# Start addresses of TensorE's operands, plain tiles in halves, and the scan's fp32 steps regrouped

## The chip, the cores and the metric

One core of a Trainium2 chip runs the whole program. The metric is the device time of one execution in microseconds (us); the kernel before took 1315.77, 1312.59 and 1308.76 us in three runs, median 1312.59. TensorE (PE) multiplies a *stationary* operand (128x128, brought in by a weight load, PEld) with a *moving* operand (128 rows by up to 512 columns), VectorE is DVE, ScalarE is ACT, GpSimd is POOL, and SyncE (SP) issues most DMAs.

## The reference

The kernel computes one Mamba-2 layer and a final RMSNorm for 512 tokens and a model width of 2048. DEPTH is 1, so the pooling mixer never runs. Cut to what matters:

```python
hn   = rmsnorm(x, ln_g)                       # (512, 2048)
proj = hn @ w_in                              # 2048 -> 10304: z (4096), x/B/C (6144), dt (64)
xbc  = silu(causal_depthwise_conv(xbc, conv_w, conv_b))      # 4 taps
dt   = softplus(dt + dt_bias);  a = -exp(a_log)
y    = ssd_chunked_scan(xs * dt, dt * a, B, C)               # 64 heads of 64, 8 groups, state 128
y    = rmsnorm((y + d_skip * xs) * silu(z), norm_g)          # over 4096
out  = rmsnorm(x + y @ w_out, final_g)                       # 4096 -> 2048
```

Everything is float32.

## The kernel before

**Splitting.** Each large product is made of fp32r matmuls. A float32 operand is split into `hi`, its fp32r rounding, made by ACT (line 85), and `lo`, the rest, made by DVE (line 86). A product takes three matmuls: hi with hi, hi with lo, lo with hi.

**Input projection.** The eight tiles of the first four pairs in `seq` ("plain") are computed directly. `mm_k` (line 192) does, for each of 16 k-tiles, three matmuls with a moving operand of 512 columns (`xh`, `xl`: the split, scaled input, all 512 tokens). The other 36 pairs of tiles go through `pair` (line 631), a Strassen-like scheme with seven products of half size. Each product (`product`, line 620) is 8 k-tiles times three matmuls with 256 moving columns; its stationary operand is a split sum of weight quarters (R11, T1, R22, T2, R21, T3, T4) and its moving operand is `xh`/`xl` or one of the forms `s` that `x_forms` makes. A pair takes QS = 28 steps, 4 to a product; the last product of a pair (T4) is returned as `last` and emitted inside the next pair, 8 steps in. The first pair has no predecessor, so nothing stands there.

**Output projection.** `opair` (line 842) does the same with y as the stationary operand (forms `f11`, `f1`, ...) and weights as the moving one, 256 columns, for two blocks of four; `mm_o` (line 881) does the rest with 512 moving columns, and the last of these stages takes its weights from the tiles named `f..` and `o..`.

**The scan** works on one unit (two heads) at a time, in fp32 matmuls and transposes between the products: `u_xt` (four transposes into the PSUM tile `tr`), `u_state` (into `yo`), `u_yd` (into `yd`, two halves of 64 columns of stationary), `u_yo` (fp32r, into `yo`), and per group of four units `g_bt` and `g_cb` (two score blocks into `tr`, masked by DVE at line 431). `tr`, `yd` and `yo` have one buffer each.

**What sets the order.** TensorE's, SyncE's and GpSimd's orders are written by hand: `run(step)` emits the functions that `add(step, f)` has put in the table `ev`, just before the matmuls of that step. The offsets are the numbers in `ramp`, in the default list `[28, 42, 56, 62, 65, 70]`, in `q_events` (loads, accumulating DMAs, splits) and in the `add` calls with `b0`. DVE's and ACT's orders come from a scheduler, with `urgent` raising a few instructions.

**Addresses.** Tiles stand in SBUF in the order in which their pools make them, padded to 32 bytes. In the built program the start addresses, modulo 256 bytes, are these:

| operands | moving | stationary | stationary minus moving | matmuls |
|---|---|---|---|---|
| `product`, 256 columns | 224 (`xh`, `xl`, `s`) | 0 (`hi`, `lo`, `h1h`, `h1l`) | 32 | 6048 |
| `oproduct`, 256 columns | 0 (`hi`, `lo`, `h1h`, `h1l`) | 224 (`f..`) | 224 | 1344 |
| `u_yo`, 256 columns | 32 | 32 | 0 | 96 |
| `mm_k`, 512 columns | 224 | 0 | 32 | 384 |
| `dt_mm`, 512 columns | 224 | 32 | 64 | 32 |
| `mm_o`, 512 columns | 0 or 224 | 0 or 224 | 0: 240, 32: 287, 224: 240 | 767 |

Adding whole k-tiles does not change the offset: their strides are multiples of 256 bytes.

Of the kernel before, what the change touches and what calls it, by code (L numbers as in the profile page):

```python
# [17 lines left out]
P = 128  # L18
L = 512
# [15 lines left out]
def mamba_layer(ctx: ExitStack, tc: tile.TileContext, d: dict, out: bass.AP):  # L35
# [14 lines left out]
    ph1 = ExitStack()  # L50
    sp = ph1.enter_context(tc.tile_pool(name="ssd", bufs=1))
    phx = ExitStack()
    xp = phx.enter_context(tc.tile_pool(name="xhat", bufs=1, side="right"))
# [112 lines left out]
    SSH = [P, 4, LH]  # L166
    xr = sp.tile([P, L + 3], F32, name="xr")

# [23 lines left out]
    def mm_k(ps, w, k8, k):  # L192
        hi, lo = w
        T.matmul(ps, hi[:, k8, :], xh[:, k, :], start=k == 0, stop=False)
        T.matmul(ps, hi[:, k8, :], xl[:, k, :], start=False, stop=False)
        T.matmul(ps, lo[:, k8, :], xh[:, k, :], start=False, stop=k == KT - 1)

# [153 lines left out]

    def dt_sums():
        pc = ps_tr.tile([P, NC, H], F32, name="tr")
        T.matmul(pc, tri, dts["a"], start=True, stop=True)
        with urgent():
            V.tensor_copy(out=cs, in_=pc)
        pl = ps_tr.tile([P, NC, H], F32, name="tr")
        T.matmul(pl, ones, dts["a"], start=True, stop=True)
        with urgent():
            V.tensor_tensor(out=nwl, in0=pl, in1=cs, op=ALU.subtract)  # L360
            V.tensor_tensor(out=win[:, 0, :], in0=nwl[:, 0, :], in1=pl[:, 1, :], op=ALU.add)
        V.tensor_copy(out=win[:, 1, :], in_=nwl[:, 1, :])
        S.activation(win, win, AF.Exp)
# [57 lines left out]
    def g_cb(g, i):  # L421
        if i == 0:
            gr[g]["cbm"] = sp.tile([P, 2, 3, P], F32, name="cbm")
        B, C = gr[g]["B"], gr[g]["C"]
        pcb = ps_tr.tile([P, 3, P], F32, name="tr")
        s0 = slice(i * 2 * P, i * 2 * P + P)
# [51 lines left out]
    def u_state(u):  # L478
# [3 lines left out]
        for c in range(2):  # L482
            T.matmul(pyo[:, 2, :], Bt[:, c, :], xw[:, c].rearrange("p h d -> p (h d)"), start=c == 0, stop=c == 1)
        with urgent():
            un[u]["sts"] = split(pyo[:, 2, :], [P, P], "sts")
# [116 lines left out]

    def q_events(n, b, last, e=0):
        for o, f, a in ((-38 - e, q_load, ("R11", 0, 0, "ra")), (-23 - e, q_split, ("R11", True)),
                        (-23 - e, q_fetch, ("T1", "R11", 0, 1)), (-3 - e // 2, q_split, ("T1",)),
                        (-12 - e // 2, q_load, ("R22", 1, 1, "rc")), (1 - e // 2, q_add, ("T2", "T1", "R22")),
# [24 lines left out]
    def pair(n, prev):  # L631
# [6 lines left out]
        W = lambda f: lambda: qs[n, f]  # L638
        product(s_, W("R11"), 11, True, b)
        A = ps_mm.tile([P, L], F32, name="mm")  # L640
        with urgent():
            S.copy(out=A[:, lo_], in_=s_)
        product(r_, W("T1"), 1, True, b + 4)
        with urgent():
            S.copy(out=sn[:, 1, :], in_=r_)  # L645
        if prev:
            prev(b + 8)
        else:
            for i in range(8, 12):
                run(b + i)  # L650
# [32 lines left out]
    for g in range(1, G):  # L683
        add(at["B", g] + (30 if ("B", g) in plain else 60), g_bt, g)
        for i in range(2):
            add(at["x", 4 * g] + 30 + 4 * i, g_cb, g, i)
    ramp = [[66, 71, 58, 75, 87, 92], [56, 65, 50, 68, 86, 92]]
    for u in range(NU):
        w = ramp[u] if u < len(ramp) else [28, 42, 56, 62, 65, 70]
        for o, f in zip(w, (u_load, u_decay, u_xt, u_state, u_yd, u_yo)):  # L690
            add(at["x", u] + o, f, u)
# [63 lines left out]
    add(b0 + 16, norm_b)  # L755
    add(b0 + 16, dt_mm)
    add(b0 + 44, g_bt, 0)
    add(b0 + 26, dt_softplus)
    add(b0 + 36, g_cb, 0, 0)
    add(b0 + 39, g_cb, 0, 1)  # L760
    add(b0 + 56, dt_sums)
    add(b0 + 62, dt_spread)

# [35 lines left out]
    def y_forms(i, j):  # L799

        n1, n2 = yraw.pop((i, j))
        if j == 0:
            for f in YF:
                yform[i, f] = [op.tile(QSH, F32R, name=f"f{f}{c}") for c in "hl"]
        jj = slice(2 * j, 2 * j + 2)
        t = fp.tile([P, 2, 2, LH], F32, name="yt")
# [35 lines left out]
    def opair(i, s, b, prev):  # L842
# [6 lines left out]
        q0, q1 = acc[:, 0:2, c[1]], acc[:, 2:4, c[1]]  # L849
        oproduct(s_, i, W("R11"), 11, True, b)  # L850
        A0 = ps_mm.tile([P, 2, LH], F32, name="mm")
        with urgent():
            S.copy(out=A0, in_=s_)
        oproduct(r_, i, W("T1"), 1, True, b + 4)
        with urgent():
            V.tensor_tensor(out=q1, in0=q1, in1=r_, op=ALU.subtract)
        if prev:
            prev(b + 8)
        else:
            for k in range(8, 12):  # L860
                run(b + k)
# [57 lines left out]
    for i, blk in enumerate(blocks):  # L919
        if type(blk) is tuple:  # L920
            for s in range(4):
                q_events(len(quads) + 4 * m + s, base[i] + s * QS, s == 3)
            for j in range(2):
# [33 lines left out]
    for kb, blk in enumerate(blocks[:-1]):  # L957
# [8 lines left out]
        for s, pairs in blk:  # L966
            ps = [None] * NC
            for p in pairs:
# [4 lines left out]
                for t in range(NC):  # L973
# [8 lines left out]
                    if p == pairs[-1]:  # L982
                        a = acc[:, t, s * L:(s + 1) * L]
                        with urgent():
                            if kb == 0 and 0 in pairs:
                                S.copy(out=a, in_=ps[t])
                            else:
                                V.tensor_tensor(out=a, in0=ps[t], in1=a, op=ALU.add)
                    if prev:
                        prev(step)  # L990
                        step += 4
                        prev = None
# [75 lines left out]
```

## Time and profile before

| | |
|---|---|
| three runs | 1315.77, 1312.59, 1308.76 us |
| profiled execution, span | 1310.4 us |
| PE busy | 1271.4 us (97%), 9548 matmul records |
| PEld busy | 1187.8 us (91%) |
| DVE busy | 1085.7 us (83%) |
| ACT busy | 832.5 us (64%) |
| DMA | 225.85 MB, mean 172 GB/s |
| granted TensorE clock | 0.995 |

The profile gives the span of its execution (first to last instruction) and no time of its own beside it; the span stands 2.2 us below the median of the runs and inside their range. The matmuls overlap in a pipeline, so a PE that is busy 97% is not at its peak. What a matmul costs in a dense stretch is the distance from its start to the next one's start, called *cadence* below; its own duration is longer, because its end is modelled with the drain of the pipeline.

### The profile page before, as it was taken

Reading aid. Unit: us, or ns where it says so; the run is one execution under the profiler, and the core shown is the slowest. Engines: PE = TensorE matmul, PEld = TensorE weight load, DVE = VectorE, ACT = ScalarE, POOL = GpSimd, SP = SyncE. Lnnn points to the kernel's source line nnn. Section 1 sums busy time; section 2 is a strip of 40 time slices with the busy share of each in tenths; the row PEclk is TensorE's granted clock in tenths of the full one; section 3 lists DMA queues with packets and bytes.
Section 4 is the critical chain, followed back from the end, with each engine's and each line's share of the span. In section 5 each row is a group of like instructions: output and inputs, shape, how many; then the busy total and the mean of one; then the engine's idle time right before and its main releaser. Section 6 shows DMA issues by size and latency. Waiting matters only on the chain.

```text
span 1310.4 us, 23695 instructions
## 1 busy us (share of the span) xinstructions
PE 1271.4 (97%) x9548; PEld 1187.8 (91%) x9548; DVE 1085.7 (83%) x1449; ACT 832.5 (64%) x1357; POOL 77.5 (6%) x99
## 2 busy tenths in 40 slices
PE   8999899999999999999999999999999999999997
PEld 6778899999999999999999999999978899799885
DVE  5787888978988897898988889888866987888855
ACT  7667667577667757766775776667765545434523
POOL 0000000010100001010000101000000000000000
PEclk9999999999999999999999999999999999999999
DMA  9536656575676657577666757756536676657602
GB/s 358 192 115 203 154 161 157 163 184 142 191 195 161 157 162 185 136 188 203 164 155 166 181 146 192 190 161 157 167 123 207 196 196 207 199 152 193 203 33 97
DMA packets 70191, 225.85 MB, mean 172 GB/s; under 512 B 8384, under 2 KB 12800, under 8 KB 69952
## 3 DMA queue, kind: packets, MB, share of 16 engines
q1 hardware_dynamic: 56688, 176.34, 40.5%
q0 software_dynamic: 12672, 46.14, 20.8%
q8 instruction: 75, 1.23, 0.4%
q10 hardware_dynamic: 720, 1.84, 0.4%
q14 instruction: 36, 0.29, 0.1%
HBM read 211.52 MB, written 12.78 MB: 171 GB/s over the span
## 4 chain that ended last, share of the span: by engine, by line
PE 67%; DVE 16%; DMA 8%; issue 5%; ACT 4%; SPq 0%; POOL 0%; DVEq 0%; ACTq 0%; POOLq 0%
PE S L627 6%; PE S L629 5%; PE S L628 5%; PE mm L627 4%; PE mm L628 4%; PE R L627 4%; PE R L629 4%; PE R L628 4%; PE mm L629 4%; DVE lo L86 4%; PE mm L838 3%; PE mm L839 3%; PE mm L840 3%; PE mm L885 2%; PE mm L887 2%
## 5 line engine op out<-in xcount | busy, mean ns | idle before, releaser
L86 DVE TENSOR_TENSOR lo<-ra,hi 128x1024 fp32r<-128x1024 f32 x150 | 180.7, 1220 | 66.1 <-ACT hi L85 62.6
L85 ACT CAST hi<-ra 128x1024 fp32r<-128x1024 f32 x150 | 155.0, 1048 | 103.8 <-PE mm L839 29.4
L627 PE MATMUL R<-s,hi 128*128 128x256 f32 x576 | 165.3, 287 | 0.7 <-ACT sn L645 0.7
L627 PE MATMUL mm<-xh,hi 128*128 128x256 f32 x576 | 165.0, 286 | 0.0
L629 PE MATMUL mm<-xh,lo 128*128 128x256 f32 x576 | 161.8, 281 | 0.4 <-DVE lo L86 0.4
L629 PE MATMUL R<-s,lo 128*128 128x256 f32 x576 | 162.1, 281 | 0.0
L628 PE MATMUL mm<-xl,hi 128*128 128x256 f32 x576 | 162.0, 281 | 0.0
L628 PE MATMUL R<-s,hi 128*128 128x256 f32 x576 | 161.7, 281 | 0.0
L85 ACT CAST hi<-rc 128x1024 fp32r<-128x1024 f32 x94 | 98.3, 1046 | 88.0 <-PE S L628 28.1
L597 DVE TENSOR_TENSOR ra<-ra,rc 128x1024 f32<-128x1024 f32 x88 | 107.4, 1220 | 18.9 <-DMA rc<-in_wi 18.3
L86 DVE TENSOR_TENSOR lo<-rc,hi 128x1024 fp32r<-128x1024 f32 x94 | 114.5, 1218 | 3.1 <-ACT hi L85 2.7
L627 PEld LDWEIGHTS mm<-xh,hi 128*128 128x128 f32 x576 | 108.6, 189 | 5.0 <-issue 5.0
L627 PEld LDWEIGHTS R<-s,hi 128*128 128x128 f32 x576 | 108.6, 189 | 1.1 <-ACT sn L645 1.1
L629 PEld LDWEIGHTS mm<-xh,lo 128*128 128x128 f32 x576 | 108.7, 189 | 0.6 <-DVE lo L86 0.6
L628 PEld LDWEIGHTS R<-s,hi 128*128 128x128 f32 x576 | 108.9, 189 | 0.0
L628 PEld LDWEIGHTS mm<-xl,hi 128*128 128x128 f32 x576 | 108.6, 189 | 0.0
L629 PEld LDWEIGHTS R<-s,lo 128*128 128x128 f32 x576 | 108.5, 188 | 0.0
L627 PE MATMUL S<-xh,h1h 128*128 128x256 f32 x288 | 84.7, 294 | 1.0 <-ACT mm L660 1.0
L627 PE MATMUL S<-xh,hi 128*128 128x256 f32 x288 | 81.7, 284 | 3.8 <-ACT xh L570 1.6
L629 PE MATMUL S<-xh,lo 128*128 128x256 f32 x288 | 81.4, 283 | 2.1 <-DVE lo L86 2.1
L628 PE MATMUL S<-xl,hi 128*128 128x256 f32 x288 | 81.1, 281 | 0.7 <-DVE xl L571 0.7
L629 PE MATMUL S<-xh,h1l 128*128 128x256 f32 x288 | 81.6, 283 | 0.0
(446 smaller groups left out, 3893.6 us busy)
## 6 DMA issues: line engine op xcount, KB each, us to landing
rc<-in_wi SPq DMA_DIRECT2D x76, 512.0 KB, 6.0
ra<-in_wi SPq DMA_DIRECT2D x42, 512.0 KB, 6.2
rb<-in_wi SPq DMA_DIRECT2D x40, 512.0 KB, 7.1
ra<-in_wi POOLq DMA_DIRECT2D x36, 512.0 KB, 7.0
rb<-in_wi POOLq DMA_DIRECT2D x36, 512.0 KB, 6.4
csb<-cscr SPq DMA_DIRECT2D x32, 512.0 KB, 8.1
ra<-in_wo SPq DMA_DIRECT2D x26, 512.0 KB, 5.1
yscr<-xs SPq DMA_DIRECT2D x32, 256.0 KB, 2.6
```

What stands on the lines that cost most here:

```text
L85: S.copy(out=hi, in_=raw)
L86: V.tensor_tensor(out=lo, in0=raw, in1=hi, op=ALU.subtract)
L597: V.tensor_tensor(out=raw, in0=raw, in1=qs[n][other], op=ALU.add)
L627: T.matmul(ps, hi[:, k, :], ah, start=first and k == 0, stop=False, skip_group_check=True)
L628: T.matmul(ps, hi[:, k, :], al, start=False, stop=False, skip_group_check=True)
L629: T.matmul(ps, lo[:, k, :], ah, start=False, stop=k == KH - 1, skip_group_check=True)
L838: T.matmul(ps[:, t, :], yh[:, k, tt], hi[:, k, :], start=st, stop=False, skip_group_check=True)
L839: T.matmul(ps[:, t, :], yl[:, k, tt], hi[:, k, :], start=False, stop=False, skip_group_check=True)
L840: T.matmul(ps[:, t, :], yh[:, k, tt], lo[:, k, :], start=False, stop=en, skip_group_check=True)
L885: T.matmul(ps, yh, hi, start=first and k == 0, stop=False)
L887: T.matmul(ps, yl, hi, start=False, stop=last and k == 1)
```

## The change

Four things, in one change:

1. **Addresses.** A 32-byte tile `edge` that nobody uses is put at the right-hand end of SBUF, `xr` grows from 515 to 560 floats per partition, and three more unused tiles (`gap` twice, 64 bytes each, `gap1`, 128 bytes) stand between others. In the built program `xh`, `xl` and the forms `s` now start at 192 modulo 256, the forms `f..` at 64, the operands that the scan makes for its large matmuls at 0 or 192, and the y operands at 0. All 8256 fp32r matmuls with 256 columns have their stationary operand 64 bytes above the moving one; of the 799 with 512 columns, 631 have offset 0 and 168 (the last stage's weights in the `f..` tiles) 192.
2. **Plain tiles in halves.** `mm_k` splits each 512-column matmul into two of 256, with the same stationary operand: 384 matmuls become 768.
3. **The scan's steps.** Both `g_cb` blocks move ahead of the transposes and write `yd` and `yo` in place of `tr`; `u_state` moves from step 62 to 65, next to `u_yd`; `u_yo` from 70 to 71; `g_bt` from 60 to 93. At the start `dt_sums` is cut in two (`dt_cumul`, `dt_sums`), and these, `dt_mm` and `dt_spread` come 2 to 6 steps later.
4. **First pair of each kind.** Where no `last` of a predecessor fills steps 8 to 11, T1's product now precedes R11's. For the first `opair` of each block T1 is split 3 steps earlier, and the `last` product that follows a block of `opair`s waits until one more tile has been emitted.

```diff
+    edge = ctx.enter_context(tc.tile_pool(name="edge", bufs=1, side="right"))
+    edge.tile([P, 8], F32, name="edge")
...
-    xr = sp.tile([P, L + 3], F32, name="xr")
+    xr = sp.tile([P, L + 48], F32, name="xr")
...
     def mm_k(ps, w, k8, k):
         hi, lo = w
-        T.matmul(ps, hi[:, k8, :], xh[:, k, :], start=k == 0, stop=False)
-        T.matmul(ps, hi[:, k8, :], xl[:, k, :], start=False, stop=False)
-        T.matmul(ps, lo[:, k8, :], xh[:, k, :], start=False, stop=k == KT - 1)
+        for n, (a, b) in enumerate(((hi, xh), (hi, xl), (lo, xh))):
+            for c in (slice(0, LH), slice(LH, L)):
+                T.matmul(ps[:, c], a[:, k8, :], b[:, k, c], start=k == 0 and n == 0 and c.start == 0,
+                         stop=k == KT - 1 and n == 2 and c.stop == L, skip_group_check=True)
...
-        pcb = ps_tr.tile([P, 3, P], F32, name="tr")
+        pcb = (ps_yo if i else ps_yd).tile([P, 3, P], F32, name="yo" if i else "yd")
...
+        if u == 0:
+            sp.tile([P, 16], F32, name="gap")
...
-                        (-23 - e, q_fetch, ("T1", "R11", 0, 1)), (-3 - e // 2, q_split, ("T1",)),
+                        (-23 - e, q_fetch, ("T1", "R11", 0, 1)), (-3 - e // 2 - t1, q_split, ("T1",)),
...
         if prev:
+            first(b)
+            second(b + 4)
             prev(b + 8)
         else:
+            second(b)
+            first(b + 4)
...
-        add(at["B", g] + (30 if ("B", g) in plain else 60), g_bt, g)
+        add(at["B", g] + (30 if ("B", g) in plain else 93), g_bt, g)
         for i in range(2):
-            add(at["x", 4 * g] + 30 + 4 * i, g_cb, g, i)
-    ramp = [[66, 71, 58, 75, 87, 92], [56, 65, 50, 68, 86, 92]]
+            add(at["x", 4 * g] + 28, g_cb, g, i)
+    ramp = [[66, 71, 63, 75, 87, 92], [56, 65, 50, 68, 86, 92]]
     for u in range(NU):
-        w = ramp[u] if u < len(ramp) else [28, 42, 56, 62, 65, 70]
+        w = ramp[u] if u < len(ramp) else [28, 42, 56, 65, 65, 71]
...
-    add(b0 + 16, dt_mm)
+    add(b0 + 18, dt_mm)
...
-    add(b0 + 36, g_cb, 0, 0)
-    add(b0 + 39, g_cb, 0, 1)
-    add(b0 + 56, dt_sums)
-    add(b0 + 62, dt_spread)
+    add(b0 + 37, g_cb, 0, 0)
+    add(b0 + 37, g_cb, 0, 1)
+    add(b0 + 59, dt_cumul)
+    add(b0 + 62, dt_sums)
+    add(b0 + 64, dt_spread)
...
-                    if prev:
+                    if prev and t > 0:
```

Here `first` is R11's product with the copy of its PSUM tile, `second` is T1's with its own; `opair` is rewritten in the same way. The order of TensorE's instructions changes as follows.

In the scan of a later group (`tr`, `yd`, `yo` are the PSUM tiles, `bc` holds B and C, `xs` the convolved x, `S` is a product's accumulator), a score block stood inside a product, after that unit's transposes:

```order
L629 MATMUL S<-xh,h1l 128x256
L428 MATMUL tr<-bc 128x2x128
L429 MATMUL tr<-bc 128x128
L627 MATMUL S<-xh,h1h 128x256
L628 MATMUL S<-xl,h1h 128x256
```

and now both blocks stand ahead of the transposes, in other tiles:

```order
L636 MATMUL S<-xh,lo 128x256
L433 MATMUL yd<-bc 128x2x128
L434 MATMUL yd<-bc 128x128
L433 MATMUL yo<-bc 128x2x128
L434 MATMUL yo<-bc 128x128
L473 MATMUL tr<-ident,xs 128x128 x4
L634 MATMUL S<-xh,h1h 128x256
```

Only the transposes still write `tr` here.

In the first `opair` of a block, T1's product (`f1`) stood directly before R22's (`f4`), which goes on in the same PSUM tile:

```order
L839 MATMUL mm<-hi,f1l 128x256
L840 MATMUL mm<-lo,f1h 128x256
L838 MATMUL mm<-hi,f1h 128x256
L839 MATMUL mm<-hi,f1l 128x256
L840 MATMUL mm<-lo,f1h 128x256
L838 MATMUL mm<-hi,f4h 128x256
L839 MATMUL mm<-hi,f4l 128x256
```

and now R11's product (`f11`, weights in `h1h` and `h1l`) stands between them:

```order
L860 MATMUL mm<-h1h,f11l 128x256
L861 MATMUL mm<-h1l,f11h 128x256
L859 MATMUL mm<-h1h,f11h 128x256
L860 MATMUL mm<-h1h,f11l 128x256
L861 MATMUL mm<-h1l,f11h 128x256
L859 MATMUL mm<-hi,f4h 128x256
L860 MATMUL mm<-hi,f4l 128x256
```

T1's product has moved 24 matmuls ahead.

In the plain tiles, the sums over dt (`bt` holds dt times a) stood one behind the other:

```order
L195 MATMUL S<-xl,hi 128x512
L196 MATMUL S<-xh,lo 128x512
L354 MATMUL tr<-bt,mask 128x256
L358 MATMUL tr<-bt,ones 128x256
L194 MATMUL S<-xh,hi 128x512
L195 MATMUL S<-xl,hi 128x512
```

and now nine pairs of halves of `mm_k` stand between the two (the first three and the last three of them are these):

```order
L357 MATMUL tr<-bt,mask 128x256
L198 MATMUL S<-xh,hi 128x256 x2
L198 MATMUL S<-xl,hi 128x256 x2
L198 MATMUL S<-xh,lo 128x256 x2
...
L198 MATMUL S<-xh,hi 128x256 x2
L198 MATMUL S<-xl,hi 128x256 x2
L198 MATMUL S<-xh,lo 128x256 x2
L363 MATMUL tr<-bt,ones 128x256
```

The first of them has also moved three k-tiles later.

More of the change, by code (lines that the diff above doesn't have):

```diff
@@ L350, in dt_softplus, with dt_cumul @@
         dts["a"] = t1
-    def dt_sums():
+    def dt_cumul():
         pc = ps_tr.tile([P, NC, H], F32, name="tr")
@@ L356, in dt_sums @@
             V.tensor_copy(out=cs, in_=pc)
+    def dt_sums():
         pl = ps_tr.tile([P, NC, H], F32, name="tr")
@@ L601, in mamba_layer, with q_events @@
     oquads = [blk for blk in blocks if type(blk) is tuple]
-    def q_events(n, b, last, e=0):
+    def q_events(n, b, last, e=0, t1=0):
         for o, f, a in ((-38 - e, q_load, ("R11", 0, 0, "ra")), (-23 - e, q_split, ("R11", True)),
-                        (-23 - e, q_fetch, ("T1", "R11", 0, 1)), (-3 - e // 2, q_split, ("T1",)),
+                        (-23 - e, q_fetch, ("T1", "R11", 0, 1)), (-3 - e // 2 - t1, q_split, ("T1",)),
                         (-12 - e // 2, q_load, ("R22", 1, 1, "rc")), (1 - e // 2, q_add, ("T2", "T1", "R22")),
@@ L638, in pair, with first, second @@
         W = lambda f: lambda: qs[n, f]
-        product(s_, W("R11"), 11, True, b)
         A = ps_mm.tile([P, L], F32, name="mm")
[L641 to L645, printed above, removed]
+        def first(step):
+            product(s_, W("R11"), 11, True, step)
+            with urgent():
+                S.copy(out=A[:, lo_], in_=s_)
+        def second(step):
+            product(r_, W("T1"), 1, True, step)
+            with urgent():
+                S.copy(out=sn[:, 1, :], in_=r_)
         if prev:
+            first(b)
+            second(b + 4)
             prev(b + 8)
         else:
+            second(b)
+            first(b + 4)
             for i in range(8, 12):
@@ L802, in y_forms @@
         if j == 0:
+            if i == 0:
+                op.tile([P, 16], F32, name="gap")
             for f in YF:
                 yform[i, f] = [op.tile(QSH, F32R, name=f"f{f}{c}") for c in "hl"]
+            if i == 0:
+                op.tile([P, 32], F32, name="gap1")
         jj = slice(2 * j, 2 * j + 2)
@@ L849, in opair, with first, second @@
         q0, q1 = acc[:, 0:2, c[1]], acc[:, 2:4, c[1]]
-        oproduct(s_, i, W("R11"), 11, True, b)
         A0 = ps_mm.tile([P, 2, LH], F32, name="mm")
[L852 to L856, printed above, removed]
+        def first(step):
+            oproduct(s_, i, W("R11"), 11, True, step)
+            with urgent():
+                S.copy(out=A0, in_=s_)
+        def second(step):
+            oproduct(r_, i, W("T1"), 1, True, step)
+            with urgent():
+                V.tensor_tensor(out=q1, in0=q1, in1=r_, op=ALU.subtract)
         if prev:
+            first(b)
+            second(b + 4)
             prev(b + 8)
         else:
+            second(b)
+            first(b + 4)
             for k in range(8, 12):
@@ L921, in mamba_layer @@
             for s in range(4):
-                q_events(len(quads) + 4 * m + s, base[i] + s * QS, s == 3)
+                q_events(len(quads) + 4 * m + s, base[i] + s * QS, s == 3, 0, 3 if s == 0 else 0)
             for j in range(2):
```

## The prediction

> **What bounds the kernel now.** I read first the busy shares and the chain of waits on the page, then the stages, then the cadence of dense stretches, then the waits of TensorE. From the page:
>
> ```profile
> PE 1271.4 (97%) x9548; PEld 1187.8 (91%) x9548; DVE 1085.7 (83%) x1449; ACT 832.5 (64%) x1357; POOL 77.5 (6%) x99
> PE 67%; DVE 16%; DMA 8%; issue 5%; ACT 4%; SPq 0%; POOL 0%; DVEq 0%; ACTq 0%; POOLq 0%
> ```
>
> TensorE is both the busiest engine and two thirds of the chain. The two large stages, the 36 pairs and the first block of `opair`s (windows: span, then busy time and instructions of PE, PEld, DVE, ACT, POOL, granted clock, DMA share, GB/s):
>
> ```profile
> 160.00:935.00 775.00, 766.31 (x6488) 744.97 (x6487) 674.85 (x865) 542.88 (x919) 57.55 (x67) 1.00 0.65 170
> 1010.00:1110.00 100.00, 97.35 (x752) 93.15 (x751) 84.90 (x101) 44.88 (x54) 6.00 (x7) 1.00 0.71 200
> ```
>
> In both, TensorE hardly pauses, the clock is full, and DVE, next, has 100 of 775 us left. So the price of one matmul decides. Five dense stretches, each set from one matmul's start to another's, same columns:
>
> ```profile
> 264.73:281.53 16.80, 16.80 (x144) 16.80 (x143) 13.29 (x16) 14.27 (x26) 1.70 (x2) 1.00 0.75 198
> 1041.96:1103.33 61.37, 61.37 (x527) 61.37 (x527) 51.12 (x56) 27.14 (x31) 4.30 (x5) 1.00 0.69 188
> 1002.58:1018.93 16.35, 16.35 (x73) 13.52 (x72) 14.57 (x22) 6.80 (x9) 0.86 (x1) 1.00 0.63 175
> 1255.72:1300.52 44.80, 44.80 (x194) 36.12 (x192) 27.58 (x59) 17.17 (x37) 0.00 (x0) 1.00 0.18 71
> 44.42:51.42 7.00, 7.00 (x32) 5.65 (x30) 6.68 (x10) 0.82 (x2) 0.00 (x0) 1.00 0.26 75
> ```
>
> A matmul still running at an edge is counted too; without these the steps are 142, 526, 72, 192 and 30. Cadences: 118.3 ns with 256 columns at offset 32 (`product`), 116.7 at 224 (`oproduct`), and with 512 columns 227.1 at offset 0, 233.3 at 32 and 233.3 at 64 (`dt_mm`). The offset acts: in one line, with the same moving tile, only the y tile differs (by-form groups: count, busy us, mean ns of one):
>
> ```profile
> L885 PE MATMUL mm<-hi,yah 128*128 128x512 f32 x68 | 27.0, 396 | 0.1
> L885 PE MATMUL mm<-hi,ybh 128*128 128x512 f32 x40 | 15.6, 390 | 0.0
> L511 PE MATMUL yo<-csth,stsh 128*128 128x256 f32 x32 | 8.9, 280 | 0.0
> L839 PE MATMUL mm<-hi,f4l 128*128 128x256 f32 x64 | 17.9, 279 | 0.0
> ```
>
> `ya` starts at 224 and `yb` at 0, the weights at 0: 6 ns apart, like the cadences. A duration is its cadence plus some 163 ns (390 - 227, 279 - 117), so `u_yo` at offset 0 (280) has 117. The three offsets seen with 256 columns lie within 2 ns; 64 was never seen in a dense stretch of these.
>
> **Cadence at offset 64, the deciding unknown.** From below: a weight load needs its own time. Four transposes of 128 columns, whose stream is half as long, take (timeline: start, length, count)
>
> ```profile
> 216.02 0.60 PE L468 MATMUL tr<-ident,xs 128*128 128x128 f32 x4
> L468 PE MATMUL tr<-ident,xs x128: 270/273/422, 88.1 to 971.0; 128*128 128x128 f32 x128
> ```
>
> (600 - 273)/3 = 109, say 110 ns each, and nothing in the trace loads 128 columns much faster. From above: the worst 512-column offsets cost one piece of 6.2 ns more than the best; one such piece on 118.3 gives 124.5. The row that speaks most against a gain is `dt_mm`: at exactly offset 64 it has the bad 233.3. [...] The nearest rows in shape are the 256-column ones, 7 ns over the floor; the excess depends on the offset, so I take the point midway from the best of them, 116.7, to the floor: 113.3. That is a choice of position, and both ends stay for the range.
>
> [...]
>
> **Sum, cadence.** `product`: 6048 x (118.3 - 113.3) = 30.2 us. `oproduct`: 1344 x (116.7 - 113.3) = 4.6. `mm_k`: 384 x (233.3 - 2 x 113.3) = 2.6; its extra 384 weight loads are in the cadence. 512 columns: of 527 `mm_o` matmuls at a bad offset 359 go to 0, with 32 of `dt_mm`: 391 x 6.2 = 2.4; the 168 that go to 192 are unmeasured (227 to 233) and kept at 233. `u_yo`, 96 x 4 ns, and the unused tiles: nothing. Together 39.8.
>
> **Sum, waits.** What TensorE and its loads wait for (us in total, times, longest):
>
> ```profile
> PEld tr L428 <- DVE xd L471: 5.9, 7, 1.8
> PE mm L838 <- DVE acc L856: 4.1, 2, 2.2
> PEld tr L354 <- ACT bt L414: 2.5, 1, 2.5
> PEld mm L838 <- ACT mm L872: 2.3, 2, 1.8
> PEld tr L358 <- DVE cs L356: 1.1, 1, 1.1
> PEld tr L315 <- DVE rbc L292: 1.0, 1, 1.0
> ```
>
> - `g_cb`: seven waits because DVE must empty `tr` of the transposes. The blocks now come first and in other buffers, whose last users ended some 13 steps earlier. 5.9 gone; the transposes behind them wait for nothing new.
> - `dt_sums`, `dt_mm`: nine matmul pairs, over 2 us, now lie before each sum, and `dt_mm` is two steps later. 2.5 + 1.1 + 1.0, of which I take 4.
> - First `opair` of each block, the one wait of 4.1:
>
> ```profile
> 1023.98 0.68 DVE L812 TENSOR_TENSOR f1l<-yt,f1h 128x512 fp32r<-128x512 f32 x1
> 1030.02 0.27 PE L840 MATMUL mm<-lo,f1h 128*128 128x256 f32 x1
> 1031.72 0.68 DVE L856 TENSOR_TENSOR acc<-acc,mm 128x512 f32<-128x512 f32 x1
> 1032.46 0.38 PE L838 MATMUL mm<-hi,f4h 128*128 128x256 f32 x1 [2.17 <-DVE acc L856]
> ```
>
> R22 waits until DVE has read T1's tile. With R11 (24 x 117 = 2.8 us) between, that reading is hidden. But `f1l` ended at 1024.66, about where T1 would now begin (1030.2 less two products of 2.8 is 1024.6), and a faster TensorE comes earlier: R11, behind it on TensorE, would wait too. I take half, 2.
> - `last` after a block: 1.3 of the 2.3, one tile more of cover.
> - `u_state` beside `u_yd`, `u_yo` at 71, `g_bt` at 93, the order of the first pair: nothing. The breaks around `u_yd` stay two a unit, and DVE's and ACT's copies for `u_yo` still have six steps (4 us). If that cover fails, `u_yo` waits about 0.5 us a unit, 16 us in all.
>
> Together 13; I count 12. **Given back:** TensorE then asks for its weights sooner. What stands behind them:
>
> ```profile
> DVE lo L86 <- ACT hi L85: 73.4, 56, 5.4
> ACT hi L85 <- PE mm L839: 63.0, 37, 3.9
> ```
>
> The splits wait for buffers that TensorE frees, so they speed up with it; DVE's share of the pair stage becomes 675/745 = 91%. Some late `lo`s will show: 6 us, a sixth of 35.
>
> 1310.4 - 39.8 - 12 + 6 = 1264.6 for the profiled span; with its 2.2 us to the median of the runs, **1267**.
>
> **Rivals.**
> 1. *The floor is reached*, 110 ns. Then 6048 x 8.3 + 1344 x 6.7 + 384 x 13.3 us/1000 + 2.4 = 66.7, less 12, and 14 given back as DVE reaches 95%: 1246 + 2 = 1248. For it: the transposes do get 109. Against: their stream is half as long, so it may collide half as often. Chance 0.21.
> 2. *DVE's splits take the place of the price.* The chain already gives DVE 16%. If half of the gain in the pairs and `opair`s returns as waits for `lo`, 17 us come back: 1284. Against: DVE's 100 us of idle time. Chance 0.12.
> 3. *Offset 64 is as good as the others*, about 117.5 with 256 columns: 6048 x 0.8 - 1344 x 0.8 - 384 x 1.7 us/1000 + 2.4 = 5.5, less 12, 1 back: 1294 + 2 = 1296. [...] For it: three offsets within 2 ns, and `dt_mm`. Chance 0.18, of which 0.06 lies within half a per cent of before because the waits come back as well.
> 4. *Slower: offset 64 collides more*, half a piece over `product`'s 118.3, 121.4 ns. Then 18.7 + 6.3 + 3.6 us more, less 2.4 and 12: 1325 + 2 = 1327. It decides from 119.6 ns on, where 8160 matmuls eat the 14.4 us won elsewhere. For it: `dt_mm` at 64 has the worse of two prices. Against: three of three offsets at 256 stay under 118.5. Chance 0.10, and 0.03 more for waits that merely cancel.
>
> That the change doesn't do what it says, I leave out: the built program's addresses show the offsets.
>
> **How the numbers follow.** The forecast has 0.36, its own range 1252 to 1282. Half a per cent, 6.6 us, is about what a measurement of this kernel can tell from no change. Faster: 0.36 + 0.21 + 0.12 + 0.12 = 0.81. Same: 0.06 + 0.03 = 0.09. Slower: 0.10. The range runs from 1238, below the floor's case with nothing given back, to 1316, just over the median before; what remains outside is mostly the fourth rival.
>
> **What would show it.** Dense stretches of `product` and `oproduct` at 111 to 115 ns say that the first step was right; 116 to 119, rival 3; over 119.6, rival 4; 110, rival 1. `mm_o` in the last stage should keep 233 where weights come from `f..` and drop to 227 elsewhere. No wait at `g_cb`, at most 2 us at both first `opair`s, and none of 2 us near 84. If DVE's share of the pair stage passes 93% with new waits of TensorE for `lo`, rival 2. I am wrong altogether if cadences fall and the span doesn't.

## The result, and the profile after

The change is real and small: 1302.1 us (median of four runs, 1301.35 to 1305.3) against 1310.67 us (median of four runs of the kernel before). The ratio is 0.9932, with a 95% interval of 0.9909 to 0.9955: 9 us, where the forecast of 1267 meant 44. The profiled span fell from 1310.4 to 1300.9 us. From the page after, the busy times and the chain of waits:

```profile
PE 1250.4 (96%) x9932; PEld 1188.6 (91%) x9932; DVE 1082.3 (83%) x1449; ACT 827.6 (64%) x1357; POOL 77.7 (6%) x99
PE 59%; DVE 15%; DMA 11%; ACT 8%; issue 6%; SPq 0%; POOL 0%; DVEq 0%; ACTq 0%; POOLq 0%
```

TensorE's share of the chain went down, from 67% to 59%; DMA rose from 8% to 11%, ACT from 4% to 8%. TensorE got faster (busy 1271.4 us before, 1250.4 now), and something else took its place in the chain. The pair stage and five dense stretches, each cut from one matmul's start to another's (span, then busy time and instructions of PE, PEld, DVE, ACT, POOL, granted clock, DMA share, GB/s):

```profile
160.00:935.00 775.00, 760.18 (x6563) 738.50 (x6561) 681.93 (x877) 547.35 (x936) 57.72 (x67) 1.00 0.65 170
595.64:614.47 18.83, 18.83 (x168) 18.83 (x167) 14.53 (x17) 13.11 (x24) 1.71 (x2) 1.00 0.92 267
810.60:841.10 30.50, 30.50 (x261) 30.50 (x260) 25.16 (x32) 18.32 (x32) 1.71 (x2) 1.00 0.82 215
1036.53:1096.14 59.61, 59.61 (x527) 59.61 (x527) 51.00 (x56) 26.55 (x30) 4.31 (x5) 1.00 0.67 184
10.74:42.42 31.68, 31.68 (x271) 31.68 (x270) 18.64 (x35) 26.54 (x42) 0.00 (x0) 1.00 0.90 356
983.40:1016.99 33.59, 33.59 (x149) 27.78 (x148) 26.90 (x44) 21.89 (x33) 0.86 (x1) 1.00 0.73 251
```

In steps of 166, 259, 526, 269 and 148 these are cadences of 113.4 and 117.8 ns for `product`, 113.3 for `oproduct`, 117.8 for the halved `mm_k`, and 226.9 with 512 columns. The same line, at the same offset 64, runs at 113.4 in one stretch and at 117.8 in another; hardly anything lies between: of 413 stretches of 12 steps of `product`, 215 have a mean under 113.8 ns, 190 one of about 117.8, and 8 lie between. ACT's and DVE's waits for the loads of `rc` (R22 and R21), and TensorE's for ACT's copies and DVE's splits, grew (us in total, times, longest). Before:

```profile
ACT hi L85 <- DMA rc<-in_wi: 22.3, 9, 3.1
DVE ra L597 <- DMA rc<-in_wi: 18.3, 13, 2.7
PE S L627 <- ACT sn L654: 1.3, 2, 0.9
PE S L629 <- DVE lo L86: 2.1, 4, 0.8
SPq L517 <- DVE xs L516: 565.4, 32, 20.5
```

and after:

```profile
ACT hi L87 <- DMA rc<-in_wi: 58.5, 23, 4.4
DVE ra L604 <- DMA rc<-in_wi: 33.5, 24, 2.9
PE S L634 <- ACT sn L670: 7.5, 7, 1.8
PE S L636 <- DVE lo L88: 4.3, 6, 1.4
PE mm L859 <- DVE acc L896: 2.9, 2, 2.3
PE mm L859 <- DVE acc L881: 2.5, 3, 1.7
SPq L524 <- DVE xs L523: 573.7, 32, 20.3
```

The waits of `g_cb` (5.9 us) have no row any more. In their place stand waits behind DMAs. The last row of each is the one that the prediction left unread: SP stands 565 to 574 us, in 32 waits, at the store of `u_yo`.

The next table is worked out from the starts of all matmuls in the two traces. A step from one start to the next counts as dense up to 1.15 times its usual length (116 ns with 256 columns, 230 with 512); what goes beyond the usual length in a longer step counts as waiting. A stage is cut at the first matmul of its kind.

| stage | before: dense + waits | after: dense + waits |
|---|---|---|
| plain tiles, ramp | 103.3 + 10.1 us | 103.3 + 11.6 us |
| pairs | 797.7 + 39.2 | 784.1 + 45.2 |
| both `opair` blocks | 159.6 + 7.5 | 158.6 + 10.6 |
| out-projection blocks | 175.6 + 1.5 | 170.1 + 1.5 |
| sum | 1236.2 + 58.3 | 1216.1 + 68.9 |

So 20.1 us came off the dense part and 10.6 us came back as waits. (The rows of the pairs and of the `opair` blocks include some 512-column matmuls of the block behind them. Each `opair` block has 6 of these before and 12 after, so 2.8 us of the out-projection blocks' 5.5 have only moved one row up.)

### The profile page after: what moved, and what is told of

It is laid out like the page before. It is cut to its first block, busy times and chain, and to the rows that moved or that the text cites. A ratio compares the mean times of both kernels' runs of the same rounds, so it can differ in the third digit from the quotient of the medians.

```text
span 1300.9 us, 24461 instructions
## 1 busy us (share of the span) xinstructions
PE 1250.4 (96%) x9932; PEld 1188.6 (91%) x9932; DVE 1082.3 (83%) x1449; ACT 827.6 (64%) x1357; POOL 77.7 (6%) x99
## 3 DMA queue, kind: packets, MB, share of 16 engines
q8 instruction: 78, 1.28, 0.4%
## 4 chain that ended last, share of the span: by engine, by line
PE 59%; DVE 15%; DMA 11%; ACT 8%; issue 6%; SPq 0%; POOL 0%; DVEq 0%; ACTq 0%; POOLq 0%
PE S L636 5%; PE S L634 5%; PE S L635 5%; PE mm L859 3%; PE mm L634 3%; PE mm L860 3%; PE mm L915 3%; PE mm L861 3%; PE mm L917 3%; PE mm L916 3%; PE R L634 3%; PE R L635 3%; PE R L636 3%; DMA ra<-in_wi 3%; DVE lo L88 3%
## 5 line engine op out<-in xcount | busy, mean ns | idle before, releaser
L87 ACT CAST hi<-ra 128x1024 fp32r<-128x1024 f32 x150 | 154.7, 1047 | 85.7 <-PE mm L860 19.7
L634 PE MATMUL R<-s,hi 128*128 128x256 f32 x576 | 160.7, 279 | 2.6 <-ACT sn L656 2.6
L87 ACT CAST hi<-rc 128x1024 fp32r<-128x1024 f32 x94 | 98.4, 1047 | 101.0 <-DMA rc<-in_wi 58.5
L635 PE MATMUL R<-s,hi 128*128 128x256 f32 x576 | 160.2, 278 | 0.0
L635 PE MATMUL S<-xl,h1h 128*128 128x256 f32 x288 | 80.6, 280 | 0.0
```

Source lines behind the costliest of these rows:

```text
L87: S.copy(out=hi, in_=raw)
L634: T.matmul(ps, hi[:, k, :], ah, start=first and k == 0, stop=False, skip_group_check=True)
L635: T.matmul(ps, hi[:, k, :], al, start=False, stop=False, skip_group_check=True)
```

## The experiments

**Two theories to tell apart.** The gain is half of the forecast in cadence, and the waits grew although the change removed some. For the cadence: either offset 64 has two states of its own, or the layer's other traffic spoils it. For the waits: either the moved steps bring them (`u_yo`'s store now reaches SP later, and the loads of the pair stand behind it), or a faster TensorE alone does.

Two places of the changed kernel show the chain in question: SP's queue, GpSimd's, then ACT, then TensorE (timeline: start, length):

```profile
323.11 0.33 SPq L524 DMA_DIRECT2D yscr<-xs  x1
323.54 0.38 SPq L81 DMA_DIRECT2D rc<-in_wi  x1
323.97 0.44 SPq L81 DMA_DIRECT2D ra<-in_wi  x1
324.50 0.38 SPq L81 DMA_DIRECT2D rc<-in_wi  x1
324.99 0.60 SPq L81 DMA_DIRECT2D rb<-in_wi  x1
...
329.14 1.05 ACT L87 CAST hi<-rc 128x1024 fp32r<-128x1024 f32 x1 [3.20 <-DMA rc<-in_wi]
...
593.00 0.33 SPq L524 DMA_DIRECT2D yscr<-xs  x1
...
594.87 0.38 SPq L81 DMA_DIRECT2D rb<-in_wi  x1
...
602.52 0.86 POOL L598 DMA_DIRECT2D rb<-in_wi  x1 [17.98 <-DMA rb<-in_wi]
...
613.14 1.06 ACT L87 CAST hi<-rb 128x1024 fp32r<-128x1024 f32 x1 [1.74 <-DMA rb<-in_wi]
614.98 1.04 ACT L87 CAST hi<-ra 128x1024 fp32r<-128x1024 f32 x1 [0.78 <-DMA ra<-in_wi]
615.93 0.36 ACT L670 COPY sn<-S 128x256 f32<-128x256 f32 x1
...
616.34 0.39 PE L634 MATMUL S<-xh,hi 128*128 128x256 f32 x1 [1.60 <-ACT sn L670]
```

At 323 us the store leaves, and four loads follow at once: they had been standing behind it. ACT then waits 3.2 us for one of them. At 593 us the same happens, and the chain can be followed to its end. The load of `rb` leaves behind the store; GpSimd, which adds a second load onto `rb`, waits 17.98 us until the first one is there; ACT waits 1.74 us for the result, and 0.78 us for a load of `ra`, in front of the copy of `S` into `sn`; and TensorE stands 1.60 us for that copy. The name in TensorE's row is a copy; the cause is a load.

### Streams without the layer

The kernel keeps only the shape of `product`, in blocks of dense matmuls:

```diff
+for k in range(8):                       # w0, w1 stationary; x0, x1 moving, 256 columns
+    matmul(acc, w0, x0); matmul(acc, w0, x1); matmul(acc, w1, x0)
+# per block one offset of w above x, modulo 256; between blocks a pause
```

> The layer is left out: only dense streams of the product's shape (two stationary tiles of 128x128, two moving tiles of 256 columns, three matmuls a step, 72 to a block), one block per offset of stationary above moving, eight offsets, with four kinds of pause between the blocks; offset 64 comes 23 times, and eight blocks of 512 columns follow. Theory: offset 64 has two modes, 113.3 and 117.8 ns, and the pause ahead of a block picks one: both cadences appear among the blocks at 64, constant inside a block, and 32 and 224 repeat 118.3 and 116.7. Rival (the layer's other traffic, DMA and copies, makes the slow mode): here all blocks at 64 run at 113.3. Second rival: where the tiles lie modulo 256, not their offset alone, decides: the seven blocks at 64 with both tiles shifted by 32 to 224 bytes differ from the others. With 512 columns: 227 at 0 and 233 at 32, 64 and 224, as the layer has them.

Four blocks (offsets 64, 64, 224 and 32; 56 steps each):

```profile
106.49:112.84 6.35, 6.35 (x58) 6.35 (x57) 0.29 (x1) 0.75 (x2) 0.00 (x0) 1.00 0.00 0
114.83:121.42 6.60, 6.60 (x58) 6.60 (x57) 0.00 (x0) 0.75 (x2) 0.00 (x0) 1.00 0.00 0
97.68:104.21 6.53, 6.53 (x58) 6.53 (x57) 0.00 (x0) 0.75 (x2) 0.00 (x0) 1.00 0.01 4
35.32:41.95 6.63, 6.63 (x58) 6.63 (x57) 0.29 (x1) 0.75 (x2) 0.00 (x0) 1.00 0.01 2
```

That is 113.3, 117.8, 116.7 and 118.3 ns: the layer's numbers, with DMA idle. The first rival falls. At 64, 12 of 22 blocks ran at 113.3 and 10 at 117.8, each constant to its end; shifting both tiles together by 32 to 224 bytes gave the same two values, so the second rival falls too. (The first block of each stream program ran its first third at over 200 ns a step, at the cadence of its offset after that, and is left out; why was not studied.) The other multiples of 32, in ns: 0: 120.0; 96: 117.3 or 118.7; 128: 118.7; 160: 120.0; 192: 117.8; 224: 116.7, once 117.8. With 512 columns: 226.7 at 0, 228.9 at 192, 232.8 to 234.3 at the other six. The pause seemed to choose in part: all five blocks behind narrow fp32 matmuls were fast.

> The layer is left out: dense streams as in the first such run, 48 matmuls a block, now with the stationary tile at 36 offsets (steps of 8 bytes, of 4 about 64), three blocks each behind a pause of narrow fp32 matmuls, of transposes and of one wide matmul; then 16 blocks with 64 for two of three matmuls and another offset for the third. Theory (two locked states of loads and streams; some phase at the start chooses): the fast state of 113.3 is seen at 64 alone of the multiples of 32; finer offsets near 64 share its two states, and at one of them all three blocks may be fast; behind the narrow matmuls 64 is fast, as it was in all five blocks of the first run. Rival (granules of 32 bytes: offsets between two multiples of 32 take the cadence of one of them): no more than eight different cadences, none under 113. A third matmul at another offset: a cadence between the two, or the slow one.

Finer offsets, three blocks each: 76 gave 113.3 three times, 52 and 88 twice each (120.0 and 116.7 the third time), 8 gave 115.6, 64 gave 113.4 once and 117.8 twice, and the rest, 60, 68 and 72 among them, lay from 116.5 to 122. 64 behind narrow matmuls was slow this time, so that pause does not choose the state: a miss. With the third matmul at another offset, 64 was never fast (117.7 to 118.9). There are more than eight cadences, and 8 (115.6) has neither that of 0 (120.0) nor that of 32 (118.3): 32 bytes are no granule of the stationary side.

> The layer is left out: dense streams as before, 48 matmuls a block, moving tiles at 192 modulo 256 as in the layer. Stationary 64, 76, 84, 88, 92, 8 and 52 bytes above them, eight blocks each behind four kinds of pause; then 64 and 76 made by moving tiles that start 20 bytes past a multiple of 32 (as in the layer's two runs at 76, where the cadence was 120.0) and 76 with moving tiles on multiples of 32; then 64 and 76 with the three matmuls of a step in another order (same moving tile first), and 64 with one matmul of 128 columns after every 24. Theory (where a moving row starts within 32 bytes counts by itself): 76 gives 113.3 with moving tiles on multiples of 32 in all blocks, and 120 with those at 20 past one. Rival (76 was fast by chance in three blocks, a state like that at 64): of eight blocks at 76 several are slow. At 64 about half of the blocks are fast; if the order of three or the added matmul chooses the state, all blocks of that kind agree.

This run was made after two runs of the layer at 76 had come out at 120 ns (below). Three of its blocks (76 on multiples of 32, 76 with the moving tiles 20 bytes past one, 52; 32 steps each):

```profile
22.69:26.32 3.63, 3.63 (x34) 3.63 (x33) 0.00 (x0) 0.37 (x1) 0.00 (x0) 1.00 0.02 5
357.38:361.22 3.84, 3.84 (x34) 3.84 (x33) 0.00 (x0) 0.37 (x1) 0.00 (x0) 1.00 0.00 0
52.05:55.68 3.63, 3.63 (x34) 3.63 (x33) 0.00 (x0) 0.37 (x1) 0.00 (x0) 1.00 0.02 5
```

113.4, 120.0 and 113.4 ns. With moving tiles on multiples of 32, 76 was fast in 7 of 8 blocks, in all 6 with the moving tiles elsewhere on such multiples, and in all 4 with the other order of three; with moving tiles 20 bytes past one, 120.0 in all 3. So where a moving row starts counts by itself. Of the other offsets, 52 was fast in all 8 blocks and 88 in 5 of 8; 84 gave 120.0, 92 gave 118.3 or 120.0, and 8 gave 115.6. 64 was fast in 1 of 7 blocks here, and in 3 of 4 with the other order. With one matmul of 128 columns added after every 24, the state changed at that matmul in all 8 blocks, 5 times from 113.3 to 117.8 ns and 3 times back. So a single odd matmul switches the state; nothing tried chooses which of the two a block starts in.

### The parts of the change

```diff
 e2_addresses = before + the unused tiles + mm_k in halves
 e3_order     = after  - the unused tiles - mm_k in halves
 e4_yo_back   = after with
-        w = ramp[u] if u < len(ramp) else [28, 42, 56, 65, 65, 71]
+        w = ramp[u] if u < len(ramp) else [28, 42, 56, 62, 65, 70]
```

> The kernel before with the addresses and the halved matmuls of the change alone (items 1 and 2), in the old order. Theory (the addresses pay some 22 us, and the moved steps gave part of it back): cadence 115 to 116 in the pairs, 113.5 in the opairs, 227 with 512 columns; starts of matmuls more than 500 ns apart stay near the 27 gaps and 31 us of before; time 1287 to 1293, so faster than the whole change. Rival (a faster TensorE alone makes the new waits, whatever the order): the gaps grow to 40 us or more and the time is 1298 to 1304.

> The change without its address tiles and halved matmuls: the new order of steps alone, at the old offsets. Theory (the moved u_yo and u_state bring the loads of the pair later, behind the store on SP's queue): the waits of g_cb, dt and the first opair go (12 us) and about as much comes back as waits for splits; time 1306 to 1314. Rival (the order is as good as forecast): 1297 to 1301.

> The change with u_state at 62 and u_yo at 70 of a unit again, as before; nothing else. Theory (the store of u_yo holds up the loads behind it on SP's queue): the loads leave 1.5 to 2 us earlier in the pair, the waits for hi and lo of the pairs shrink by 8 to 14 us, time 1288 to 1294. Rival 1 (TensorE waits at u_yo for the copies of the state, which the move covered): 0.3 to 0.5 us more a unit, time 1305 to 1318. Rival 2 (the step makes no difference): 1300 to 1304.

| kernel | time, us | ratio to before (95%) | `product`, mean ns | pairs: dense + waits |
|---|---|---|---|---|
| before | | 1 | 118.3 | 797.7 + 39.2 |
| the change | 1302.1 | 0.9932 (0.9909 to 0.9955) | 115.4 | 784.1 + 45.2 |
| addresses alone | 1309.6 | 0.9975 (0.9957 to 0.9992) | 116.4 | 786.3 + 38.8 |
| order alone | 1312.4 | 1.0001 (0.9987 to 1.0015) | 118.3 | 801.3 + 36.2 |
| `u_yo` back at 70, `u_state` at 62 | 1293.1 | 0.9850 (0.9825 to 0.9876) | 115.7 | 783.2 + 36.8 |

The order alone is worth nothing, as its theory said. Putting back two numbers, the steps of `u_state` and `u_yo`, takes the changed kernel from 0.9932 to 0.9850 of before. The waits on the loads of `rc` (58.5 us in the change) follow the order, not the cadence. With the addresses alone they are

```profile
ACT hi L87 <- DMA rc<-in_wi: 17.3, 8, 3.9
```

with the order alone

```profile
ACT hi L85 <- DMA rc<-in_wi: 55.8, 21, 4.7
```

and with `u_yo` back at 70

```profile
ACT hi L87 <- DMA rc<-in_wi: 13.1, 9, 2.1
```

The run of the addresses alone missed both expectations. Its waits in the pairs fitted the theory, and its cadence nearly (116.4, where 115 to 116 was expected), but its ramp took 123.6 us, not 113.4, with one wait of 5.2 us for the first unit's decay tile:

```profile
PE yd L500 <- DVE m L459: 5.2, 1, 5.2
```

In the middle of that tile ACT turns to an activation of `bc` and loads tables three times (1.28 us each), against once in the kernel before; why the rest of the ramp stretched is open. In the change itself the ramp took 114.9 us. The `opair` blocks wait 11.5 us with the addresses alone and 7.2 with the order alone (7.5 before, 10.6 in the change): there the new waits follow the cadence. The order alone has a price of its own: `u_state` beside `u_yd` takes 16.8 us from start to start over its 128 matmuls, against 12.1 before (and 11.8 with `u_yo` and `u_state` put back).

### The store on SP's queue

```diff
+    def u_store(u):
+        nc.sync.dma_start(yscr[u // UPG][:, u % UPG, :], un[u]["y"])
 ...
-        nc.sync.dma_start(yscr[u // UPG][:, u % UPG, :], y)      # in u_yo
 ...
+        add(at["x", u] + w[5] + 7, u_store, u)
```

> The change with one edit: the store of u_yo's result is issued seven steps later, so that on SP's queue the loads of the next pair stand ahead of it; u_yo stays at 71. Theory (the store, waiting for DVE, holds up the loads behind it): the waits of the pair stage shrink from 45 us to 36 or less, time 1284 to 1294. Rival (the moved u_yo and u_state delay DVE's and ACT's own work on the splits, and SP has no part): waits of 43 us or more, time 1299 to 1304.

> The same late store with u_state at 62 and u_yo at 70, as before. Theory: the loads were held up in the kernel before, too, so the waits fall below the 36.8 us of the run with u_yo back: 1280 to 1290. Rival (at 70 the loads are early enough, or their buffers come free no sooner): 1291 to 1296. Second rival (one more buffer of y held for longer delays the convolution that needs it): above 1297.

> The new order of steps with the late store, at the offsets of before, mm_k whole. Theory (the store is what held the loads, at any cadence): the waits of the pair stage fall from 36 us to 25 to 30, time 1299 to 1306; against it the late store at offset 64 is worth 17 to 22 us, which is then what the addresses are worth when TensorE isn't held up by loads. Rival (with a slower TensorE the loads came early enough): waits stay at 33 to 36 us, time 1309 to 1313.

With the store seven steps later the changed kernel took 1281.5 us, 0.9750 of before (0.9734 to 0.9766); with `u_yo` at 70, 1283.6 us, 0.9769 (0.9754 to 0.9783). At the old offsets it took 1299.1, 0.9897 (0.9877 to 0.9917). All three fell on the theory's side, the first by more than it had said. The addresses are thus worth 1.5% with the loads freed (0.9897 to 0.9750), and 0.7% without (1.0001 to 0.9932). The chain of the first, from its page:

```profile
PE 85%; DVE 6%; DMA 5%; ACT 2%; issue 1%; SPq 0%; DVEq 0%; ACTq 0%
```

and two of its waits:

```profile
ACT hi L87 <- DMA rc<-in_wi: 0.7, 1, 0.7
SPq L538 <- DVE xs L523: 52.8, 5, 13.5
```

The waits for `rc` are all but gone, SP stands 52.8 us at the store and no longer 573.7, and TensorE has 85% of the chain. The pairs' waits are 26.5 us, of 45.2. Its loads leave one by one, as their buffers come free, and no longer as a bunch:

```profile
298.65 0.42 SPq L538 DMA_DIRECT2D yscr<-xs  x1
299.13 0.42 SPq L440 DMA_DIRECT2D csb<-cscr  x1
...
306.71 0.34 SPq L81 DMA_DIRECT2D rc<-in_wi  x1
307.10 0.43 SPq L81 DMA_DIRECT2D ra<-in_wi  x1
315.95 0.33 SPq L81 DMA_DIRECT2D rc<-in_wi  x1
322.02 0.33 SPq L81 DMA_DIRECT2D rb<-in_wi  x1
```

In the kernel before, the bunch stands behind the store as well:

```profile
323.65 0.33 SPq L517 DMA_DIRECT2D yscr<-xs  x1
324.08 1.19 SPq L79 DMA_DIRECT2D rc<-in_wi  x1
325.32 0.42 SPq L79 DMA_DIRECT2D ra<-in_wi  x1
```

So the store held up the loads there too. What that cost isn't shown: no run has the kernel before with the late store alone. With the new order at the old offsets the late store is worth 1.0% (1.0001 to 0.9897).

### The forecast's cadence, in the layer

Two runs put the weights 76 bytes above the moving tiles by moving the latter, with and without the late store:

```diff
-    xh = xp.tile([P, KT, L], F32R, name="xh")
+    xa = xp.tile([P, 2 * KT * L + 64], F32R, name="xa")    # xh, xl: slices that start 5 floats in
```

> The late store, and the moving tiles (normed x and its forms) 12 bytes lower, so that the weights stand 76 bytes above them and not 64 (product and the halved mm_k; oproduct stays at 64). Theory (at 76 the streams lock into 113.3 whatever came before, as in three blocks of three): product's mean cadence falls from 116.1 to 113.4, the dense part of the pair stage by about 17 us to 771, and since hardly a wait was left there, most of it stays: time 1262 to 1270. Rival 1 (in the layer a disturbance throws the streams out of the fast state at 76, too): mean cadence over 115, time 1277 to 1282. Rival 2 (DVE's splits become the bound): cadence 113.4 but 8 us or more of it back as waits for hi and lo, time 1272 to 1278.

> The change as it is, with u_yo at 71 and the store in its place, but the weights 76 bytes above the moving tiles. It asks what the change would have brought if the cadence had been the forecast 113.3. Theory (the store holds up the loads, so the pair is no longer set by TensorE's cadence): product at 113.4, but half or more of the 13 us returns as waits, time 1292 to 1299. Rival (the waits do not depend on the cadence): 1286 to 1290.

Both expectations fell: 1306.7 us, 0.9963 of before (0.9945 to 0.9981), and 1319.2 us, 1.0061 (1.0037 to 1.0084). `product` ran at 120.0 in both, with no other state; the third stream run (above) was made to see why, and shows it. A stretch of 245 steps of the first:

```profile
255.56:284.96 29.40, 29.40 (x248) 29.40 (x246) 24.87 (x31) 20.73 (x34) 1.71 (x2) 1.00 0.68 189
```

This is the prediction's fourth rival, brought about by another offset: with an unlucky start address the changed kernel is slower than the one before (1.0061).

The next two shift the weights instead, by 12 bytes, in one tile that serves as a ring of three `hi` and three `lo` slots (R11's weights, one product of seven, stay at 64):

```diff
+    hilo = wp.tile([P, 6 * 2 * L + 64], F32R, name="hilo", bufs=1)
+        at = (n % 3 * 2 * L + 3, (3 + (n + 1) % 3) * 2 * L + 3)      # hi, lo of the n-th split
```

> The late store with u_yo at 71, and the weight tiles hi and lo of the products 12 bytes higher (76 above moving tiles that stay on multiples of 32); R11's own tiles, one product of seven, and oproduct stay at 64. Theory (76 made by the stationary side locks at 113.3 in the layer as in 17 of 18 such blocks): mean cadence of product 113.4 to 114.0, against 116.1 with the late store alone, 13 to 16 us less in the pair stage; hardly a wait is left there, so most of it stays: 1265 to 1273. Rival 1 (DVE's splits become the bound): the cadence falls and half of it comes back as waits for hi and lo, 1274 to 1279. Rival 2 (in the layer something throws the streams out of the fast state): mean over 115.5, 1279 or more.

> The change as it is (store in its place, u_yo at 71) with hi and lo 12 bytes higher, so that product runs at the forecast's 113.3 to 114. Theory (the store holds up the loads, so part of the pair is set by them and not by TensorE's cadence): of the 9 to 10 us that the cadence takes off the 115.4 of the change, half or more returns as waits in the pair stage (over 49 us there, against 45.2): 1295 to 1300. Rival (the forecast's sum holds once its cadence holds, waits unchanged): 1289 to 1293.

In both, splits from the last pair on overwrote tiles still in use, so their total times (1299.3 and 1326.6 us) say nothing of the cadence, and they are read between the first transposes of units 4 and 28 alone, which came earlier. `product` ran at 113.7 and 113.6 there: the forecast's number. Time of these 24 units, dense and waits, from the starts of the matmuls:

| `product` | store in its place | store seven steps later |
|---|---|---|
| 120.0 ns | 688.2 = 672.7 + 15.5 | 685.1 = 672.7 + 12.4 |
| 118.3 (old offsets, new order) | 682.3 = 664.1 + 18.2 | 677.1 = 664.1 + 13.0 |
| 115.4 and 116.1 (the offsets of the change) | 677.9 = 648.9 + 29.0 | 668.0 = 653.2 + 14.8 |
| 113.6 | 675.1 = 640.5 + 34.6 | 660.7 = 640.5 + 20.2 |

The first column is the answer to where the gain went. From 118.3 to 113.6 the dense part falls by 23.6 us, and the time by 7.2: 16.4 us come back as waits. With the loads ahead of the store the same step brings 16.4 us. The late store is worth more the faster TensorE runs: 3.1, 5.2, 9.9 and 14.4 us down the table.

> As the run with the late store and hi and lo 12 bytes higher, but a split into the shared ring of weight tiles is issued only behind the last product that reads the tile it replaces. (In that run and its partner the splits at the change from the pairs to the out projection overwrote tiles still in use, which changed the result and added some 15 us of waits there; units 4 to 28 of the scan were untouched, and took 660.7 us against 668.0 without the shift.) Theory (the cadence of 113.4 pays what it paid in those units, about 7 us, and 1 more in the ramp): 1270 to 1277. Rival (the waits come back with the faster TensorE in the other stages): 1278 to 1284.

With the ring in order it took 1278.9 us, 0.9745 of before (0.9729 to 0.9761): within the interval of the late store alone, a miss by 2 us against its theory, and in the range of its rival. Units 4 to 28 took 661.4 us, where the table has 660.7; `product` ran at 113.6, a stretch of 94 steps of it:

```profile
597.51:608.17 10.66, 10.66 (x95) 10.66 (x95) 10.63 (x13) 8.44 (x15) 0.45 (x1) 1.00 0.60 143
```

Against the late store alone these units won 6.6 us, and the rest lost about as much: the ramp 0.6, the other pairs 3.2, the out-projection blocks 1.4, and the `opair`s 1.3, where `oproduct`, still at 64, ran at 116.4 on average and not at 114.7. In the stretch shown DVE is busy for 10.63 of 10.66 us, but over units 4 to 28 for 596.6 of 661.4, 90%, and no row has TensorE waiting there for one of DVE's splits.

## Why the prediction was wrong

It forecast 45.8 us off the profiled span, and 9.5 came. Of the missing 36.3 us, 19.7 are dense time (39.8 forecast, 20.1 found) and 16.6 are waits (6 off, 10.6 more).

- **Cadence at offset 64.** 113.3 was right as a state and wrong as a mean. `product` ran at 115.4: 6048 x 2.9 = 17.5 us for the forecast 30.2. The step that failed is "the point midway", which took an unknown for one number. It has two, 113.3 and 117.8, and the third rival (117.5) and the forecast were each right in half of the stretches. That the midpoint fell on the lower of the two to a tenth of a nanosecond is luck: no row of the prediction pointed to it. So is the mean of 115.4, which depends on how the states fell: other kernels at 64 had up to 116.4. That the two states need no traffic of the layer, the streams show: with DMA idle, 12 of 22 blocks at 64 ran at 113.3 and 10 at 117.8.
- **`oproduct`**: 113.9 on average, 3.8 us for 4.6: right, but luck has a part in it, since in the other runs at 64 it was anything from 113.8 to 117.7.
- **`mm_k` in halves**: 117.1 on average, so two halves take 234.2 against 233.3; nothing for the forecast 2.6. The ramp's dense time did not move.
- **512 columns**: 226.9 at 0, as forecast. At 192, where the forecast kept 233 and named that as a sign, the 168 matmuls ran at 229.2 in the change itself (228.9 in the stream run): about 0.7 us more gain than counted.
- **Moved steps at "nothing".** This is the second step that failed. `u_state` beside `u_yd` cost 4.7 us by itself (12.1 to 16.8, in the order alone), about half of it as waits. With `u_state` and `u_yo` both put back, the waits in the pairs fall by 8.4 us (45.2 to 36.8); 2.7 of these lie in `u_state`'s steps, and the rest is not split further, since no run moved `u_yo` alone. Their cause is the store, which stands on SP's queue ahead of the pair's loads: with both steps left where they are and only the store later, the waits fall to 26.5 us. The prediction looked for the copies of the state as `u_yo`'s cover, and named a price of 16 us if that failed; it didn't follow the instruction's own DMA to its queue, although SP's waits stood in the trace.
- **Waits removed, 12.** `g_cb`'s 5.9 us went, as forecast. The rest did not come, because most of the waits moved to another place. In the ramp the waits went from 10.1 to 11.6 us: the sums wait no longer, but TensorE now waits 3.8 us for a split near 79 us. With the order alone, at the old cadence, that split costs 2.6 us and the ramp's waits are 10.4, so it isn't the faster TensorE alone. In the first `opair` of the first block the wait at R22 (2.2 us) is gone, but 0.8 and 1.4 us for the split of T2 and 2.3 at T3, until DVE has read T2's tile, have taken its place; the order alone shows the same two waits for the split (0.9 and 1.4). In the second block 1.7 us are left at R22. The `last` behind the second block waits 1.1 us, of 1.3; with the order alone, nothing. Both blocks together wait 3.1 us more.
- **Given back, 6.** In the pairs 11.9 us came back (45.2 against 39.2 less 5.9), 2.4 of them in `u_state`'s steps. The mechanism, that TensorE then asks for its weights sooner, was right (in units 4 to 28, 16.4 of 23.6 us of dense time came back as waits); the limiter was misread. The forecast had splits behind DVE's share of the time, and that share was 88% (681.93 of 775), under the 93% it had set. The limiter was the order on a queue, loads held up by a store (45.2 us of waits, 26.5 with the store later), and not the amount of DVE's work. The prediction had also read from PE's busy time (766.31 of 775 us) that TensorE hardly pauses; by the starts of its matmuls the pairs had 39.2 us of waits.
- **The rivals.** DVE's splits taking the place (second rival) is not what happened in the change; with the loads freed and 113.6 ns, DVE's share rises to 90%, without such a wait. The third rival's 117.5 is near the upper one, 117.8, at which nearly half of `product` ran. "The floor" of 110 ns, worked out from the transposes of 128 columns, was seen in no stream of 256: the lowest cadence at any of 36 offsets was 113.3. That 110 ns bounds such a stream from below was the author's estimate; no run shows the bound.

## What to carry to other kernels

When a step moves, follow every instruction it issues to the queue on which it stands, and read what stands behind it there: here a store that waited for its data held back the loads behind it (SP stood 573.7 us at such stores, in 32 waits), and TensorE's row named a copy. A gain in cadence is kept only as far as the loads can come earlier; test that by freeing them, because the same late store was worth 5.2 us at 118.3 ns and 14.4 at 113.6. An unknown that depends on an address is not a number between two bounds: measure it as a stream by itself before it carries the sum, and expect more than one state, as at 64 (113.3 and 117.8).

## What the runs showed of the hardware

- The cadence of 256-column fp32r matmuls with 128x128 weights depends on where the weights start against the moving tile, modulo 256 bytes: 113.3 to 122 ns over 36 offsets, in streams with DMA next to idle (share 0.00 to 0.02 in the blocks shown). With moving tiles on multiples of 32, the only multiple of 32 with a state under 116.5 is 64.
- At 64 there are two states, 113.3 and 117.8 ns (12 and 10 of 22 blocks), kept without change from one interruption to the next; one added matmul of 128 columns switched the state in all 8 blocks that had it. 76 kept to 113.3 in 16 of 17 such blocks of these two stream runs (3 of 3, and 13 of 14 with the same order of three), and at 113.6 on average in the layer.
- A moving tile 20 bytes past a multiple of 32 gave 118.9 at offset 64 and 120.0 at 76, in all 3 blocks each, and 120.0 at 76 in the layer. Weights 12 bytes past such a multiple (76, moving tiles on one) ran at 113.3. Why a moving row's start counts so, no run shows.
- The best version found is the change with its store seven steps later: 1281.5 us, 2.5% under the kernel before; with the weights 12 bytes higher it is 1278.9 us, which the measurement does not tell from it.
